# Modulation products in groups of four on TensorE, and other places in the order for three kinds of transfers

## The chip, the core and the metric

The kernel runs on one core of a Trainium2 chip. The core has a matrix engine (TensorE, PE in the profile, its weight loads as PEld), a vector engine (VectorE, DVE), an activation engine (ScalarE, ACT), a general engine (GpSimd, POOL) and a queue engine (SyncE, SP). Sixteen DMA engines move data between HBM and the on-chip memory SBUF; in this kernel transfers are issued from SP and from POOL. Products are accumulated in PSUM, from which DVE and ACT read. The metric is the device time of one execution in microseconds; lower is better.

## The reference

One inference step of a two-layer decoder trunk over a prompt of 1024 tokens and 8 single-token samples that share the weights (model width 1024). Cut to what matters here:

```python
for l in range(2):
    mod = silu(c) @ ada_w[l] + ada_b[l]              # c: 1 prompt row and 8 sample rows
    sh1, s1, g1, sh2, s2, g2 = split(mod, 6)         # each 1024 wide
    h = rmsnorm(x, norm_mix[l]) * (1 + s1) + sh1
    out, state = even_mixer(h) if l == 0 else mamba_mixer(h)
    x = x + g1 * out
    h = rmsnorm(x, norm_mlp[l]) * (1 + s2) + sh2
    x = x + g2 * (square(relu(h @ mlp_w1[l])) @ mlp_w2[l])      # hidden width 4096
y = rmsnorm(x, norm_final)
```

The even mixer has four HGRN2 heads of 128 channels, a gated linear recurrence. For the samples a head takes one recurrent step on a given state, once per sample:

```python
S = f[:, None] * S + (1 - f)[:, None] * v[None, :]   # S: 128 x 128 per head and sample
o = q @ S                                            # the new S is an output too
```

## The kernel before, in words

**Number format and large products.** Data is float32. A large product is made of three matmuls of rounded halves (lines 395 to 397, `mm3`): weight-high by data-high, weight-high by data-low, weight-low by data-high. `prep` loads a weight unit of 128x1024 on SP (`raw`, two buffers), ACT rounds it (`whi`) and DVE takes the rest (`wlo`); `need` hands out the next unit and keeps three more in preparation.

**Order.** The program is written as one sequence. The framework then places every instruction on its engine by a simulated schedule of its own, in which an instruction goes as soon as its inputs are there in the simulation; on the chip each engine then runs its list strictly in order. `tc.keep_in_program_order(i)` puts an instruction behind the one written just before it on the same engine. `dma` issues a transfer on SP; `dma_aux` (line 199) issues it on POOL and always pins it, so POOL's transfers keep the written order, and a transfer that has to wait holds all behind it. `Background` runs generators a step at a time between products, so that small work is written in between large work.

**Modulation** (`ada_gen`, line 251). Per layer three groups `g`, each of eight slices `k`. One slice is a group of four products, `j` = 0 to 3: the condition tile `ct` (128x32) is the weight, a tile of `ada_w` (128x512 float32, 256 KB) the data, and the result goes to 32 rows of one PSUM tile, so each `j` uses other 32 columns of the array. The float32 product shows as two MATMUL records on line 272. `load()` issues the four tiles of a slice on SP, one slice ahead; after eight slices ACT copies the sum (line 278), PE transposes it (line 281), DVE writes `mod`. `ada_steps(n)` advances the generator by n steps: 10 at the start, one with each weight unit that `need` hands out in the even mixer, 3 and then one with each of the first 16 products of the first half of an MLP, and one with each unit of its second half. Layer 1's modulation is made in layer 0's MLP; its last group (`g` = 2, `rest=1` holds back its first load) falls into the second half.

**MLP, first half** (from line 710). The hidden layer is computed with a seven-product scheme (Strassen's, Winograd's form) on 16 pairs `p` of weight tiles: `AOPS` lists 112 products `(p, q)`. Each is 24 matmuls into one of four PSUM tiles `pd`; DVE takes it out by lines 748 to 770, by `q`. Products 1 and 2 of the pairs in `SPLIT` (0 to 7, 14 and 15) run early, and product 1 of these is stored to HBM (`keep`, line 745) and loaded back (`kept`, line 704, into `saved`) for line 748, which is part of `q` = 6. `ff_out` (line 670) makes relu and square of a finished tile on ACT, splits it (lines 577 and 578), and stores it to `fd` in HBM on POOL. From pair 2 on the order within a pair is 6, 7, 5, 4, 3 (with 1 first and 2 after 5 where they did not run early). After products (14, 1) to (15, 2) come pairs 12 and 13 with all seven, then 14 and 15 with five each.

**MLP, second half** (line 783). Eight chunks of four `w2` units. A chunk reads eight tiles `ffc`, which `load_ff` loads from `fd` on POOL. Those of chunk 0 are loaded during the last 24 products of the first half, one with each product, into buffers (tag `hA`) that products 1 and 2 read until (13, 2).

**HGRN head** (`hgrn_gen`, line 825). For the first half of the tokens and the samples: `vd` (line 901) writes the samples' v to HBM in pieces of 4 bytes, `vb` (line 932) reads it back copied to all partitions; then for each half of the samples 256 KB of the old state `stt` is loaded (line 947), scaled by `f` on ACT (line 951), and added to on DVE (line 952); the result is stored (line 961). All this is issued on SP. Around it PE transposes (lines 898, 906), ACT copies (903, 908) and PE goes on with line 913.

Of the kernel before, what the change touches and what calls it, by code (L numbers as in the profile page):

```python
# [7 lines left out]
F32 = mybir.dt.float32  # L8
# [138 lines left out]
def kernel(ctx: ExitStack, tc: tile.TileContext, A: dict):  # L147
# [25 lines left out]
    def t2(w=W2, dt=F32):  # L173
        t = tp.tile([P, W2], dt, name="t2", tag="t2", bufs=N2)
        return t[:, :w]
# [20 lines left out]
    def dma(out, in_):  # L196
        nc.sync.dma_start(out=out, in_=in_)
# [53 lines left out]
    def ada_gen(l, alloc, rest=None):  # L251


        todo = [(12 * l + 4 * g, k) for g in range(3) for k in range(KT)]
        raws = []

        def load():
            if todo:
                i, k = todo.pop(0)
                rs = [alloc(512) for _ in range(4)]  # L260
                for j, raw in enumerate(rs):
                    dma(raw, A["ada"][i + j][:, k * 512:k * 512 + 512])
                raws.append(rs)
        load()
        yield
        for g in range(3):
            pt = psm()
            if not raws:
                load()
            for k in range(KT):  # L270
                for j, raw in enumerate(raws.pop(0)):
                    PE.matmul(pt[32 * j:32 * j + 32], ct[:, k], raw, start=k == 0, stop=k == KT - 1,
                              tile_position=(0, 32 * j))
                if (g, k) != (rest, KT - 1):
                    load()
                yield
            st = alloc(512)
            S.copy(st, pt)
            pm = psm()
            for q in range(4):  # L280
                PE.transpose(pm[:, q * P:q * P + P], st[:, q * P:q * P + P], ident)
            i0 = 48 * l + 16 * g
            V.tensor_add(mod[:, i0:i0 + 16, :].rearrange("p (j q) b -> p j q b", q=4),
                         pm.rearrange("p (q j b) -> p j q b", q=4, j=4)[:, :, :, 0:9],
                         vec("adab", i0, 16).rearrange("p (j q) -> p j q", q=4).unsqueeze(3)
                         .broadcast_to([P, 4, 4, 9]))
            yield
# [92 lines left out]
    def need(kind, idx):  # L380

        i = wpos[0]
        assert order[i] == (kind, idx), (i, order[i], kind, idx)
        wpos[0] += 1
        if kind[0] != "a":
            ada_steps(1)
        while len(units) <= min(i + AHEAD, max(i, limit[0] - 1)):
            units.append(prep(*order[len(units)]))
        u, units[i] = units[i], None
        return u  # L390
# [270 lines left out]
    def mlp(l, ctx_b, res, last, lorder=(3, 2)):  # L661
# [42 lines left out]
        def kept(p):  # L704

            if p in SPLIT and p not in saved:
                saved[p] = t3(HX)
                dma_aux(saved[p], keep[p])
# [5 lines left out]
        for i, (p, q) in enumerate(AOPS):  # L714
# [15 lines left out]
                stage[0] = None  # L730
            if q == 6:
                kept(p)
            elif q == 4 and p + 1 in keep:
                kept(p + 1)
            w = 512 * (n % 2), got[n // 2]
            m1, m2 = pair_tiles(p)
            pt = pd()
# [34 lines left out]
            if (p, q) == FRONT[1][-1]:  # L772
                ff0 = load_ff(0)
                ffs = next(ff0)
            elif ffs:
                next(ff0, None)
            bg.tick(2)
            if i < 2 * LEAD:
# [46 lines left out]
    def hgrn_gen(h, hf, st, carry, ff):  # L825

        n = HALF_N[hf]
        v4 = lambda a: a.rearrange("p (a t) -> p a t", t=P)
        v8 = lambda a: a.rearrange("p (a t) -> p a t", t=64)

        f = st.pop("f")
        V.tensor_scalar(f, f, lbo[:, h:h + 1], lbt[:, h:h + 1], op0=ALU.mult, op1=ALU.add)
# [65 lines left out]
            PE.transpose(pt[:, sb * P:sb * P + P], vt[:, sb * P:sb * P + P], ident)  # L898
        if hf == 0:
            vd = dr.tile([NS, P], F32, name="vd", tag="vd", bufs=2)  # L900
            dma(vd.rearrange("b p -> p b"), vt[:, 512:520])
        vn = vt[:, :512]
        S.copy(vn, pt)
        pt = psm()
# [20 lines left out]
                                       op0=ALU.mult, op1=ALU.add)  # L925
            carry["S"] = Sn
        if hf == 1:
            dma(A["o_hgp"][h], carry["S"])
        if hf == 0:
            vb = [t2(512), t2(512)]  # L930
            for qq in range(2):
                dma(vb[qq], vd[4 * qq:4 * qq + 4].rearrange("(o b) p -> o (b p)", o=1).broadcast_to([P, 512]))
        yield
        po = psm()
        for sb in range(4):
# [5 lines left out]
        yield  # L941
        if hf == 0:

            stts = []
            for qq in range(2):
                stt = t2(512)
                dma(stt, A["st_hg"][h][:, qq * 512:qq * 512 + 512])
                for bb in range(4):
                    b = 4 * qq + bb
                    c = slice(bb * P, bb * P + P)  # L950
                    S.mul(stt[:, c], stt[:, c], fs[:, b:b + 1])
                    V.scalar_tensor_tensor(stt[:, c], vb[qq][:, c], fs[:, 8 + b:9 + b], stt[:, c],
                                           op0=ALU.mult, op1=ALU.add)
                stts.append(stt)
                yield
            pq = psm()
            for b in range(NS):
                PE.matmul(pq[:, b:b + 1], stts[b // 4][:, (b % 4) * P:(b % 4) * P + P], qs[:, b:b + 1],
                          start=True, stop=True)
            for qq in range(2):  # L960
                dma(A["o_hgs"][h][:, qq * 512:qq * 512 + 512], stts[qq])
            S.copy(o[:, 512:520], pq[:, 0:8])

        while "g" not in st:
# [784 lines left out]
```

## Time and profile before

| | us |
|---|---|
| median of 3 runs | 2911.93 |
| lowest and highest | 2908.77 and 2917.14 |
| profiled execution | 2907.54 |
| its span, first to last instruction | 2905.8 |

In the profile's rows, "x" is a count, "<-" names what ended a wait or, between tile names, what was read for what was written. "busy" of PE counts a matmul until its modelled end, so matmuls overlap in it. A row of the view of waits gives the waiting engine, the line, what it waited for, the total in us, the times and the longest. A row of the timeline gives the start in us, the length, engine, line, operation, tiles, shapes and count, and in brackets the idle time before it and what ended it. A row of the view of stretches gives the stretch, its length, each engine's busy us with its count of instructions, PE's granted clock (1.00 is full), the DMA engines' busy share and GB/s.

The stages by the trace: the even mixer to about 570 us, layer 0's MLP to 1350 (first half to 961), the odd mixer to 2180, layer 1's MLP to the end (first half to 2527).

### The profile page before, as it was taken

To read this page: it belongs to the slowest core of one execution; us is meant where nothing else is said; L and a number is where in the kernel's file an instruction comes from. 1 tells how busy PE (TensorE), PEld (TensorE's weight loads), DVE (VectorE), ACT (ScalarE), POOL (GpSimd) and SP (SyncE) were. 2 spreads that over 40 slices of the span, in tenths; PEclk is the share of its full clock that TensorE was granted. 3 is DMA by queue.
4 is the path that set the end of the run, shared out by engine and by line. 5 is a ranking of instruction groups with operands and counts; after the bars stand their busy time and mean duration, and the time that the engine had idled before them with its cause. 6 is when DMAs were issued, how large, how long until landed. Compare 5 with 4: busy or idle time off the path is not lost. (4 is left out here: it accounts for less than half of the span.)

```text
span 2905.8 us, 47220 instructions
## 1 busy us (share of the span) xinstructions
PE 2771.9 (95%) x18636; PEld 2445.0 (84%) x18636; DVE 1854.9 (64%) x3712; ACT 1390.6 (48%) x2347; POOL 208.2 (7%) x356
## 2 busy tenths in 40 slices
PE   7999899999998899999889999999999999899998
PEld 3777788768998789999889897787779999899997
DVE  5646553666776334447689788998778766544446
ACT  4665522364555200015688776878756556301002
POOL 0000000011111200100000000000002111301100
PEclk9999999999999999999999999999999999999999
DMA  8642301296656943431656546443335655844431
GB/s 296 176 152 68 95 31 59 100 307 193 194 171 208 338 136 113 160 112 54 121 134 190 143 135 159 138 136 120 113 116 175 194 160 168 280 172 161 168 102 66
DMA packets 199933, 444.23 MB, mean 153 GB/s; under 512 B 35488, under 2 KB 53792, under 8 KB 199712
## 3 DMA queue, kind: packets, MB, share of 16 engines
q1 hardware_dynamic: 138144, 277.92, 32.2%
q0 software_dynamic: 61568, 163.29, 16.9%
q8 instruction: 147, 2.41, 0.3%
q14 instruction: 74, 0.61, 0.1%
HBM read 343.06 MB, written 98.08 MB: 152 GB/s over the span
## 5 line engine op out<-in xcount | busy, mean ns | idle before, releaser
L376 ACT CAST whi<-raw 128x1024 fp32r<-128x1024 f32 x228 | 238.1, 1046 | 826.3 <-PE pg L396 804.8
L505 DVE SCALAR_TENSOR_TENSOR x<-pg,mod,x 128x256 f32<-128x256 f32 (+1 forms) x576 | 326.3, 570 | 433.9 <-PE pg L397 428.5
L395 PE MATMUL pg<-hh,whi 128*128 128x264 f32 (+2 forms) x1656 | 546.5, 330 | 11.2 <-ACT xy L1203 5.4
L396 PE MATMUL pg<-hl,whi 128*128 128x264 f32 (+2 forms) x1656 | 533.2, 322 | 0.1
L397 PE MATMUL pg<-hh,wlo 128*128 128x264 f32 (+2 forms) x1656 | 532.8, 322 | 0.0
L395 PE MATMUL pg<-ffc,whi 128*128 128x256 f32 (+2 forms) x1488 | 476.9, 320 | 1.7 <-ACT t L577 1.7
L397 PE MATMUL pg<-ffc,wlo 128*128 128x256 f32 (+2 forms) x1488 | 477.6, 321 | 0.0
L396 PE MATMUL pg<-ffc,whi 128*128 128x256 f32 (+2 forms) x1488 | 476.6, 320 | 0.0
L377 DVE TENSOR_TENSOR wlo<-raw,whi 128x1024 fp32r<-128x1024 f32 x228 | 278.2, 1222 | 168.6 <-ACT whi L376 140.5
L395 PEld LDWEIGHTS pg<-hh,whi 128*128 128x128 f32 x1656 | 314.2, 190 | 53.7 <-issue 13.8
L396 PEld LDWEIGHTS pg<-hl,whi 128*128 128x128 f32 x1656 | 314.2, 190 | 31.5 <-issue 6.4
L397 PEld LDWEIGHTS pg<-hh,wlo 128*128 128x128 f32 x1656 | 313.5, 189 | 26.1 <-issue 2.1
L395 PE MATMUL pd<-hh,whi 128*128 128x258 f32 x1024 | 294.9, 288 | 26.2 <-DVE t L748 21.5
L395 PEld LDWEIGHTS pg<-ffc,whi 128*128 128x128 f32 x1488 | 280.5, 189 | 31.5 <-ACT whi L376 5.0
L397 PEld LDWEIGHTS pg<-ffc,wlo 128*128 128x128 f32 x1488 | 280.0, 188 | 25.3 <-issue 2.7
L396 PEld LDWEIGHTS pg<-ffc,whi 128*128 128x128 f32 x1488 | 279.8, 188 | 22.5 <-issue 0.2
L396 PE MATMUL pd<-hh,whi 128*128 128x258 f32 x1024 | 293.5, 287 | 0.0
L397 PE MATMUL pd<-hh,wlo 128*128 128x258 f32 x1024 | 291.6, 285 | 0.0
L395 PEld LDWEIGHTS pd<-hh,whi 128*128 128x128 f32 x1024 | 196.3, 192 | 42.3 <-issue 33.5
L396 PEld LDWEIGHTS pd<-hh,whi 128*128 128x128 f32 x1024 | 196.1, 191 | 12.0 <-issue 9.5
L397 PEld LDWEIGHTS pd<-hh,wlo 128*128 128x128 f32 x1024 | 196.4, 192 | 2.5 <-issue 2.5
L395 PE MATMUL pg<-ffh,whi 128*128 128x264 f32 (+2 forms) x544 | 176.4, 324 | 2.7 <-ACT bcz L1387 1.8
(291 smaller groups left out, 5299.8 us busy)
## 6 DMA issues: line engine op xcount, KB each, us to landing
raw<-W SPq DMA_DIRECT2D x314, 512.0 KB, 4.2
ffc<-fd POOLq DMA_DIRECT2D x128, 516.0 KB, 10.6
fd<-x POOLq DMA_DIRECT2D x106, 516.0 KB, 4.1
t<-ada SPq DMA_DIRECT2D x192, 256.0 KB, 5.2
t<-csd SPq DMA_DIRECT2D x64, 256.0 KB, 4.8
fd<-t POOLq DMA_DIRECT2D x44, 258.0 KB, 4.9
x<-xd POOLq DMA_DIRECT2D x16, 516.0 KB, 9.9
t<-st_ss SPq DMA_DIRECT2D x32, 256.0 KB, 4.5
```

The source lines that it names most:

```text
L376: S.copy(hi, raw)
L377: V.tensor_sub(lo, raw, hi.bitcast(F32))
L395: PE.matmul(pt, wh, xh, start=first and i == 0, stop=False)
L396: PE.matmul(pt, wh, xl, start=False, stop=False)
L397: PE.matmul(pt, wl, xh, start=False, stop=last and i == n - 1)
L505: V.scalar_tensor_tensor(x[:, m, s:s + npr], pt[:, :npr], mod[:, self.gi + m, 0:1], x[:, m, s:s + npr], op0=ALU.mult, op1=ALU.add)
```

## The change

It has five parts.

1. The four products of a slice are written in the order `j` = 3, 0, 1, 2, and the last three are pinned behind the one written before.
2. `ada_steps` is not called with the first eight units of an MLP's second half, so that layer 1's last modulation group begins with chunk 2 in place of chunk 0.
3. `kept`: the load for pair p+1 is written at product (p, 6) and no longer at (p, 4), and only for p above 1. For p = 2 the load stands at (2, 6) itself, together with that for pair 3; before, it stood at (1, 4). A load at (0, 4) whose result was read by nothing is gone.
4. The eight `ffc` tiles of chunk 0 are loaded with every second product and no longer with each.
5. In a HGRN head the old state is one tile of 512 KB (`hst`, one buffer), loaded at the head's beginning; it, `vd`, `vb`, the new state (now one store) and the prompt's end state are issued on POOL. ACT's and DVE's work on the state is the same, written to the one tile.

```diff
@@ -268,9 +268,12 @@
             for k in range(KT):
-                for j, raw in enumerate(raws.pop(0)):
-                    PE.matmul(pt[32 * j:32 * j + 32], ct[:, k], raw, start=k == 0, stop=k == KT - 1,
-                              tile_position=(0, 32 * j))
+                rs = raws.pop(0)
+                for j in (3, 0, 1, 2):
+                    mm = PE.matmul(pt[32 * j:32 * j + 32], ct[:, k], rs[j], start=k == 0, stop=k == KT - 1,
+                                   tile_position=(0, 32 * j))
+                    if j < 3:
+                        tc.keep_in_program_order(mm)
@@ -382,7 +385,7 @@
-        if kind[0] != "a":
+        if kind[0] != "a" and (kind[:2] != "w2" or idx >= 8):
             ada_steps(1)
@@ -730,8 +733,8 @@
             if q == 6:
                 kept(p)
-            elif q == 4 and p + 1 in keep:
-                kept(p + 1)
+                if p > 1 and p + 1 in keep:
+                    kept(p + 1)
@@ -772,7 +775,7 @@
-            elif ffs:
+            elif ffs and i % 2:
                 next(ff0, None)
@@ -827,6 +830,9 @@
+        if hf == 0:
+            stt = ph.pool.tile([P, NS * P], F32, name="hst", tag="hst", bufs=1)
+            dma_aux(stt, A["st_hg"][h])
@@ -898,7 +904,7 @@
-            dma(vd.rearrange("b p -> p b"), vt[:, 512:520])
+            dma_aux(vd.rearrange("b p -> p b"), vt[:, 512:520])
@@ -925,11 +931,11 @@
         if hf == 1:
-            dma(A["o_hgp"][h], carry["S"])
+            dma_aux(A["o_hgp"][h], carry["S"])
         if hf == 0:
             vb = [t2(512), t2(512)]
             for qq in range(2):
-                dma(vb[qq], vd[4 * qq:4 * qq + 4].rearrange("(o b) p -> o (b p)", o=1).broadcast_to([P, 512]))
+                dma_aux(vb[qq], vd[4 * qq:4 * qq + 4].rearrange("(o b) p -> o (b p)", o=1).broadcast_to([P, 512]))
@@ -941,24 +947,18 @@
-            stts = []
             for qq in range(2):
-                stt = t2(512)
-                dma(stt, A["st_hg"][h][:, qq * 512:qq * 512 + 512])
                 for bb in range(4):
                     b = 4 * qq + bb
-                    c = slice(bb * P, bb * P + P)
+                    c = slice(b * P, b * P + P)
                     S.mul(stt[:, c], stt[:, c], fs[:, b:b + 1])
-                    V.scalar_tensor_tensor(stt[:, c], vb[qq][:, c], fs[:, 8 + b:9 + b], stt[:, c],
+                    V.scalar_tensor_tensor(stt[:, c], vb[qq][:, bb * P:bb * P + P], fs[:, 8 + b:9 + b], stt[:, c],
                                            op0=ALU.mult, op1=ALU.add)
...
-            for qq in range(2):
-                dma(A["o_hgs"][h][:, qq * 512:qq * 512 + 512], stts[qq])
+                PE.matmul(pq[:, b:b + 1], stt[:, b * P:b * P + P], qs[:, b:b + 1], start=True, stop=True)
+            dma_aux(A["o_hgs"][h], stt)
```

More of the change, by code (lines that the diff above doesn't have):

```diff
@@ L942, in hgrn_gen @@
         if hf == 0:
-            stts = []
             for qq in range(2):
-                stt = t2(512)
-                dma(stt, A["st_hg"][h][:, qq * 512:qq * 512 + 512])
                 for bb in range(4):
                     b = 4 * qq + bb
-                    c = slice(bb * P, bb * P + P)
+                    c = slice(b * P, b * P + P)
                     S.mul(stt[:, c], stt[:, c], fs[:, b:b + 1])
-                    V.scalar_tensor_tensor(stt[:, c], vb[qq][:, c], fs[:, 8 + b:9 + b], stt[:, c],
+                    V.scalar_tensor_tensor(stt[:, c], vb[qq][:, bb * P:bb * P + P], fs[:, 8 + b:9 + b], stt[:, c],
                                            op0=ALU.mult, op1=ALU.add)
-                stts.append(stt)
                 yield
@@ L957, in hgrn_gen @@
             for b in range(NS):
-                PE.matmul(pq[:, b:b + 1], stts[b // 4][:, (b % 4) * P:(b % 4) * P + P], qs[:, b:b + 1],
-                          start=True, stop=True)
-            for qq in range(2):
-                dma(A["o_hgs"][h][:, qq * 512:qq * 512 + 512], stts[qq])
+                PE.matmul(pq[:, b:b + 1], stt[:, b * P:b * P + P], qs[:, b:b + 1], start=True, stop=True)
+            dma_aux(A["o_hgs"][h], stt)
             S.copy(o[:, 512:520], pq[:, 0:8])
```

## The prediction, made before the changed kernel was run

> **What bounds the kernel now.** I read the page first: the sum per engine, then the view of PE's waits.
>
> ```profile
> span 2905.8 us, 47220 instructions
> PE 2771.9 (95%) x18636; PEld 2445.0 (84%) x18636; DVE 1854.9 (64%) x3712; ACT 1390.6 (48%) x2347; POOL 208.2 (7%) x356
> ```
> ```profile
> PE pd L395 <- DVE t L748: 23.0, 4, 9.6
> PE psm L913 <- ACT t L908: 15.0, 2, 9.0
> PE psm L272 <- DMA t<-ada: 12.6, 7, 4.8
> ```
>
> PE is the bound, 95% busy, with every other engine far below. What can go is PE's idle time, 2905.8 - 2771.9 = 134 us, and PE work that is arranged badly. Three of the largest waits are at places that the change touches: line 748 (kept products), line 913 (a HGRN head, behind ACT) and line 272 (modulation tiles not landed). PE's own price per product is read from its timeline, a lone modulation product first, then a whole group of four (two records each), and from a stretch without any:
>
> ```profile
> 577.48 0.39 PE L395 MATMUL pd<-hh,whi 128*128 128x258 f32 x1
> 577.79 1.04 PE L272 MATMUL pm<-t,ct 128*32 128x512 f32 x2
> 578.77 0.39 PE L396 MATMUL pd<-hh,whi 128*128 128x258 f32 x1
> ```
> ```profile
> 625.26 0.28 PE L397 MATMUL pd<-hh,wlo 128*128 128x258 f32 x1
> 625.48 1.06 PE L272 MATMUL pm<-t,ct 128*32 128x512 f32 x8
> 626.48 0.39 PE L395 MATMUL pd<-hh,whi 128*128 128x258 f32 x1
> ```
> ```profile
> 574.00:668.00 94.00, 93.28 (x523) 54.98 (x524) 60.75 (x81) 54.73 (x87) 16.13 (x29) 0.98 0.94 312
> 14.00:40.00 26.00, 24.07 (x87) 6.12 (x88) 6.56 (x19) 5.69 (x12) 0.00 (x0) 1.00 0.98 360
> 970.00:990.00 20.00, 15.98 (x58) 7.16 (x59) 3.01 (x5) 1.05 (x1) 6.36 (x12) 0.84 1.10 403
> 790.00:840.00 50.00, 49.79 (x416) 49.61 (x415) 31.22 (x50) 28.32 (x50) 6.86 (x10) 1.00 0.56 163
> ```
>
> Without modulation a matmul takes 49.79/416 = 0.12 us, a seven-product step of 24 takes 2.87. With the lone product the next start comes 578.77 - 577.48 = 1.29 after the one before, with the group of four 626.48 - 625.26 = 1.22; less 0.12 they cost 1.17 and 1.10. Four products beside each other cost what one costs: **1.15 us a piece, however many of a group stand in it**.
>
> **Part 1, groups of four.** The pieces are counted in PE's timeline; the first and the last of two stretches:
>
> ```profile
> 45.30 2.38 PE L272 MATMUL psm<-t,ct 128*32 128x512 f32 x6
> ...
> 201.58 1.04 PE L272 MATMUL psm<-t,ct 128*32 128x512 f32 x2
> ...
> 574.04 3.51 PE L272 MATMUL pm<-t,ct 128*32 128x512 f32 x6 [2.91 <-DVE x L604]
> ...
> 662.65 4.11 PE L272 MATMUL pm<-t,ct 128*32 128x512 f32 x10
> ```
>
> From 45 to 203 there are 21 pieces for 14 groups, from 574 to 668 34 for 16. The pins make 0, 1 and 2 follow 3, whose tile is issued last, so each group becomes one piece. Even mixer: seven pieces fewer; that at 45 lies beside PE's start, where it waits for its data anyway, so 6 x 1.15 = **6.9 us**. First half of the MLP: 18 x 1.15 = 20.7 us of PE work goes. But there the cover is thin: the DMA engines are at share 0.94. The stretch moves 94 x 312 = 29.3 MB. At the 403 GB/s of the row from 970 this takes 72.7 us, at the 360 of the row from 14 81.4, at its own 312 per 0.94, so 332, 88.3. The gain lies between 94 - 88.3 = 5.7 and the whole 20.7; I take the row from 14, which carries the same tiles: **12.6 us**. What is late next there is a tile of `ada`.
>
> **Part 2, the last group of layer 1.** In chunk 0 PE meets tiles just issued, while the DMA engines are at share 1.10:
>
> ```profile
> 972.35 3.81 PE L272 MATMUL psm<-t,ct 128*32 128x512 f32 x4 [4.79 <-DMA t<-ada]
> 976.10 0.58 PE L397 MATMUL pg<-ffc,wlo 128*128 128x256 f32 x1
> ...
> 984.30 1.05 PE L272 MATMUL psm<-t,ct 128*32 128x512 f32 x4
> ...
> 989.05 0.39 PE L395 MATMUL pg<-ffc,whi 128*128 128x256 f32 x1
> ```
>
> The wait of 4.79, then 976.10 - 972.35 - 0.98 = 2.8 within the first piece (0.98 is a piece's own length, 577.79 to 578.77), then 989.05 - 984.30 - 0.98 = 3.8 in the second group: 11.4 us. The first slice is in three pieces, so 2 x 1.15 more goes. In chunk 2 the first slice is again loaded in the same step as its products, but the burst of loads that opens the second half is over (the calm stretch from 790 has share 0.56); a wait there is between 0 and 4.8, I take half: 11.4 + 2.3 - 2.4 = **11.3 us**.
>
> **Parts 3 and 4, kept products and `ffc`.** Layer 0 on POOL, DVE and PE:
>
> ```profile
> 914.31 1.63 POOL L201 DMA_DIRECT2D ffc<-fd  x3 [30.08 <-PE pd L397]
> ```
> ```profile
> 932.23 0.70 DVE L578 TENSOR_TENSOR x<-t,x 128x516 fp32r<-128x516 f32 x1 [2.59 <-ACT x L577]
> 934.94 0.70 DVE L578 TENSOR_TENSOR x<-t,x 128x516 fp32r<-128x516 f32 x1 [2.01 <-ACT x L577]
> ...
> 936.92 1.90 DVE L373 TENSOR_TENSOR wlo<-t,whi 128x512 fp32r<-128x512 f32 x3
> 940.13 0.69 DVE L748 TENSOR_TENSOR t<-t,pd 128x516 f32<-128x516 f32 x1 [1.32 <-DMA t<-kept]
> ```
> ```profile
> 940.97 0.55 PE L395 MATMUL pd<-hh,whi 128*128 128x258 f32 x1 [9.59 <-DVE t L748]
> 941.32 0.42 PE L396 MATMUL pd<-hh,whi 128*128 128x258 f32 x1
> 941.53 0.42 PE L397 MATMUL pd<-hh,wlo 128*128 128x258 f32 x1
> ```
>
> POOL stands 30 us with the first `ffc` load at its head, which needs the buffer of (13, 2); all behind it goes out in a burst, and pair 14's kept load is the fifteenth in it, behind eight `ffc` and six `fd`. It lands at 940.13: (940.13 - 914.31)/15 = 1.72 us a place. By the new written order (`ffc` with odd products, the kept load at (13, 6), not (13, 4)) it is the ninth, at about 930. The wait of POOL stays. DVE is late itself, though: the two `L578` wait for stores that free their slots, in the eighth and tenth place before, the fifth and seventh after, some 5 us earlier. Without the kept load DVE is free at 936.92 + 1.90 = 938.8; 5 us earlier it starts line 748 near 934.6 instead of 940.13. I take **5.5 us** per layer (the view of waits has the same row in layer 1: 23.0 in 4, two of them near 9.6), between 1.3 (DVE no earlier) and the whole 9.6. After the wait PE runs slower: 0.21 us a matmul, not 0.12, for one product of 24, 2.2 us. By the Trainium skill, "TensorE: Matmul & The Clock Gate", Part 1 (What's actually happening), an idle window of about 3.4 us drops PE to half its clock; the trace agrees (0.21 to 0.12). By this rule the 4 us of wait that I leave would still cost these 2.2, and only a wait cut below 3.4 would add 2 x 2.2 to the gain; the sum takes nothing.
>
> Against this stands the load for pair 2, now at its own product. Layer 1:
>
> ```profile
> 2271.80 1.38 POOL L201 DMA_DIRECT2D fd<-x  x2 [5.04 <-DVE x L578]
> ```
> ```profile
> 2276.72 0.28 PE L395 MATMUL pd<-hh,whi 128*128 128x258 f32 x1
> ```
> ```profile
> DMA to landing us min/median/max: 2.8/4.7/10.0
> ```
>
> It comes behind these two stores, at about 2272.9, and lands by the kept loads' median at 2277.6. DVE waits at line 748 with all its queue; PE needs that tile of four at its 31st product, 2276.72, and gets it at 2277.6 + 0.7 + 0.1. 1.7 us, and I take 1.8 per layer, between 0 and 7 (the longest landing). Pairs 3 to 7 get their loads earlier and had no wait. Together 2 x (5.5 - 1.8) = **7.4 us**.
>
> **Part 5, HGRN heads.**
>
> ```profile
> ACT t L951 <- DMA t<-st_hg: 16.0, 2, 9.0
> ```
> ```profile
> 144.05 0.38 SPq L197 DMA_DIRECT2D vd<-t  x1
> 144.53 2.58 SPq L197 DMA_DIRECT2D t<-ada  x4
> ```
> ```profile
> 155.99 5.36 PE L272 MATMUL psm<-t,ct 128*32 128x512 f32 x8 [4.67 <-DMA t<-ada]
> ```
>
> In heads 2 and 3 ACT waits 16.0 us in all for the state, which SP issues only after `vd` has landed; the copies of lines 903 and 908 stand behind it, and PE at line 913 behind these, 15.0 us. Loaded at the head's start, the state is there, and what is left is a copy of 0.6 each: **13.8 us** (lower bound 7, if DVE, which still waits for `vb` at line 952, delays ACT; upper 18 with the slow clock after). Six issues per head come to POOL, idle in this stage; new waits there (`vb` for `vd`, a state for the store before it) hold only each other.
>
> In head 1 four `ada` loads are issued right behind `vd` and PE waits 4.67 and then within the piece 5.36 - 1.06 = 4.3. Moved to another queue, `vd` may leave these loads free or not; no POOL transfer stands beside a `vd` in this trace. Between 0 and 9.0 I take half, **4.5 us**.
>
> **Sum**: 6.9 + 12.6 + 11.3 + 7.4 + 13.8 + 4.5 = 56.5 us off the profiled execution's 2907.5. It lies 4.4 us under the median of 2911.9, from which I take the sum: **2855 us**, 2.0%.
>
> **The rivals.** *`vd` clogs all engines wherever it is issued*: its 4-byte pieces hold the 16 engines, the 4.5 stays, and `vb` comes no earlier, so DVE in heads 2 and 3 gives half of 13.8 back: 2911.9 - (56.5 - 4.5 - 6.9) = 2867. For it: one set of 16 engines is all there is to share. The Trainium skill says so, "DMA: Bandwidth & Descriptors", Issuing engines are not separate DMA queues: issuing elsewhere saves only issue time. No run here shows it yet.
>
> *Transfers set the pace from 574 to 668*: 5.7 in place of 12.6 there, only 8.9 in chunk 2 (a wait of 4.8), 1.3 per layer in place of 5.5, no 4.5: 2911.9 - (6.9 + 5.7 + 8.9 - 1.0 + 13.8) = 2878. For it speaks the share of 0.94, against it the whole group at 625, beside which PE had no wait.
>
> *The change doesn't do what it says*: a pin gives an order, not a neighbour, and other matmuls slip in between. Then 6.9, 12.6 and 2.3 go: 2877. The chain 3, 0, 1, 2 leaves little room for it: once 3 is placed, the other three are ready.
>
> *Slower: PE waits for the last of four tiles.* Before, each product went when its own tile was there; now PE stands until the fourth of a group has landed, and all four buffers come free at once, so the next loads start late. Place: the 38 groups behind PE's start. It decides from 56.5/38 = 1.5 us a group; at 2.0 the time is 2911.9 - 56.5 + 76 = 2931. For it speaks that PE waited 12.6 us for such tiles already; against it that groups of eight records, as at 625, stand in the trace without a wait.
>
> **How the numbers follow.** Forecast 0.52, clogging 0.13, transfers 0.12, not together 0.05, gains mostly given back by new waits (within 0.3%, about what a measurement of this kernel can tell from no change, 8.7 us) 0.09, slower 0.09. Faster 0.82, same 0.09, slower 0.09. With every term at its upper bound (6.9 + 20.7 + 13.7 + 19.2 + 18 + 9.0) the time is 2824, with every one at its lower (6.9 + 5.7 + 8.9 - 11.4 + 7 + 0) 2895; this is the range, and it leaves out the last two cases.
>
> **What would show it.** Right: modulation pieces of eight records throughout, fewer than 50 of them; no `DMA t<-st_hg` among ACT's waits, line 913 under 2 us; line 272 not at 972; PE's wait for line 748 near 4 us instead of 9.6 in both layers, and a new one of 1 to 3 us about four products after (2, 6). Wrong: waits of PE for `ada` that grow past 20 us, DVE waiting at line 952 so that weights come late, or a stretch from the even mixer's end to i = 16 that is as long as before with PE idle in it.

## The result and the profile after

| | before | after |
|---|---|---|
| median, us | 2913.69 | 2897.45 |
| lowest and highest of 4 runs | 2908.77 and 2917.14 | 2892.55 and 2900.79 |
| profiled execution, us | 2907.54 | 2900.04 |

The ratio is 0.9944, 95% interval 0.9921 to 0.9967: faster, by 16 us where 56.5 were forecast; the time lies 2 us above the upper end of the range. One execution of `rows_no_1_5`, 8994 us, and one of the kernel before in the runs further down, 5405 us, were in a slow state and are left out of the ratios. The first lines of the profile's page after the change, then rows of its view of PE's waits (engine, line, what ended the wait, us in total, times, longest; lines 273, 398 and 751 are 272, 395 and 748 of before):

```profile
span 2898.2 us, 47219 instructions
PE 2743.0 (95%) x18636; PEld 2448.9 (84%) x18636; DVE 1855.8 (64%) x3712; ACT 1390.0 (48%) x2346; POOL 221.0 (8%) x378
```
```profile
PE psm L273 <- DMA t<-ada: 20.8, 8, 9.6
PE pm L273 <- DMA t<-ada: 15.5, 8, 3.7
PE pd L398 <- DVE t L751: 12.0, 7, 3.1
PE pg L398 <- issue: 9.6, 2, 5.3
PE pd L398 <- ACT whi L375: 7.0, 4, 3.3
PE psm L919 <- ACT t L914: 2.5, 2, 2.0
```

PE is busy 28.9 us less (2771.9 before), yet the span shrinks by only 7.6: saved work became waiting. The wait at line 748 fell from 23.0 to 12.0 and that behind the HGRN copies from 15.0 to 2.5; the one for tiles of `ada` rose from 12.6 to 20.8 + 15.5 = 36.3. By stages, each from the first matmul of one to that of the next, read from both timelines (the two profiled executions are 7.5 us apart where the medians are 16, so the stages explain half of what was measured):

| stage, us | before | after | gain | forecast |
|---|---|---|---|---|
| start to layer 0's first product (even mixer) | 577.5 | 575.5 | 2.0 | 6.9 + 13.8 + 4.5 |
| products 0 to 16, layer 0 | 90.4 | 89.2 | 1.2 | 12.6 |
| product 16 to second half, both layers | 293.6 + 297.9 | 297.9 + 300.9 | -7.3 | 7.4 |
| second half, layer 0 | 389.4 | 377.1 | 12.3 | 11.3 |

The rest (odd mixer, layer 1's first products and second half) differs by 0.7 us. One stage came as forecast, three did not: the even mixer lacks 23.2 us of its forecast, the products from 16 on 14.7, and products 0 to 16 11.4.

**Products 0 to 16.** The view of stretches (us, PE, PEld, DVE, ACT, POOL busy with counts, granted clock, DMA share, GB/s), and one of the new waits in PE's timeline:

```profile
574.00:665.00 91.00, 74.69 (x523) 54.68 (x516) 60.06 (x78) 52.63 (x83) 16.36 (x29) 0.88 0.92 313
580.00:660.00 80.00, 65.64 (x473) 50.03 (x472) 51.66 (x66) 45.93 (x70) 15.81 (x28) 0.91 0.97 330
```
```profile
647.39 1.06 PE L273 MATMUL pm<-t,ct 128*32 128x512 f32 x8 [2.29 <-DMA t<-ada]
648.38 0.52 PE L398 MATMUL pd<-hh,whi 128*128 128x258 f32 x1
648.70 0.42 PE L399 MATMUL pd<-hh,whi 128*128 128x258 f32 x1
648.91 0.42 PE L400 MATMUL pd<-hh,wlo 128*128 128x258 f32 x1
...
655.55 1.93 PE L273 MATMUL pm<-t,ct 128*32 128x512 f32 x8 [3.23 <-DMA t<-ada]
```

The 16 groups stand in 15 pieces, where 34 were. In the starts of successive matmuls, modulation takes 17.8 us of PE in place of 35.5, and idle time 16.3 in place of 0.7. Between 580 and 660 the DMA engines are at 0.97, and the tiles come no faster. They are also asked for late. SP's issues of the tiles that PE waits for at 647.39 and 655.55, and a row of SP's waits from 575 to 665:

```profile
642.27 2.88 SPq L197 DMA_DIRECT2D t<-ada  x4
648.46 9.36 SPq L197 DMA_DIRECT2D t<-ada  x6
```
```profile
SPq L197 <- PE pm L273: 24.0, 14, 3.5
```

The first load of each row goes out as soon as a group of PE (those that start at 641.19 and 647.39 and last 1 us) has freed its buffer. The tiles waited for at 647.39, 655.55 and 661.17, 9.2 of the 15.5 us, were issued within 0.5 us of the end of the group before, and landed 3.6 to 6.6 us later.

**Even mixer.** SP's and POOL's issues, and the DMA view's lines of the two kinds of small stores (tile, queue, count, KB each, median us from issue to landing):

```profile
155.84 0.90 POOL L201 DMA_DIRECT2D vd<-t  x1 [13.24 <-ACT sm L245]
166.55 1.09 POOL L201 DMA_DIRECT2D t<-vd  x2 [9.81 <-DMA vd<-t]
```
```profile
156.60 0.33 SPq L197 DMA_DIRECT2D raw<-W  x1
157.03 8.57 SPq L197 DMA_DIRECT2D t<-ada  x6
```
```profile
bcd<-bcz SPq DMA_DIRECT2D x8, 4.0 KB, 14.3
vd<-t POOLq DMA_DIRECT2D x4, 4.0 KB, 10.1
```

4 KB take 10 us, and the `ada` tiles that SP issues in that time land only at 171.7 to 173.5; PE waits 9.59 us for them at 173.57. The queue was changed, the sixteen engines are the same. The DVE view holds what became of ACT's wait for the state:

```profile
DVE hst L955 <- DMA t<-vd: 16.9, 3, 8.7
```

**End of the first half.** POOL's timeline in layer 0:

```profile
916.46 0.55 POOL L201 DMA_DIRECT2D ffc<-fd  x1 [30.07 <-PE pd L400]
...
921.23 0.85 POOL L201 DMA_DIRECT2D t<-kept  x1
```
```profile
935.03 0.36 PE L398 MATMUL pd<-hh,whi 128*128 128x258 f32 x1 [1.50 <-DVE t L751]
...
941.40 0.39 PE L398 MATMUL pd<-hr,whi 128*128 128x258 f32 x1 [3.26 <-ACT whi L375]
...
942.56 0.58 PE L400 MATMUL pd<-hr,wlo 128*128 128x258 f32 x1 [0.65 <-DVE wlo L376]
```
```profile
938.70 0.69 DVE L340 TENSOR_TENSOR t<-raw 128x512 f32<-128x512 f32 x1 [3.01 <-DMA raw<-W]
```

Pair 14's kept load goes out in the ninth place, as forecast, and the wait of 9.59 is now 1.50. But a weight unit's load lands late (DVE's row), so PE waits for that unit (3.26 + 0.65), and the second half starts 4.28 late: 9.7 us in all.

### The profile page after: what moved, and what is told of

It is laid out like the page before. It is cut to its first block, busy times and chain, and to the rows that moved or that the text cites. A ratio compares the mean times of both kernels' runs of the same rounds, so it can differ in the third digit from the quotient of the medians.

```text
span 2898.2 us, 47219 instructions
## 1 busy us (share of the span) xinstructions
PE 2743.0 (95%) x18636; PEld 2448.9 (84%) x18636; DVE 1855.8 (64%) x3712; ACT 1390.0 (48%) x2346; POOL 221.0 (8%) x378
## 3 DMA queue, kind: packets, MB, share of 16 engines
q0 software_dynamic: 63456, 169.34, 17.7%
## 5 line engine op out<-in xcount | busy, mean ns | idle before, releaser
L398 PE MATMUL pg<-hh,whi 128*128 128x264 f32 (+2 forms) x1656 | 545.9, 330 | 11.5 <-ACT whi L379 4.4
```

The lines of the kernel that those rows point to most:

```text
L398: PE.matmul(pt, wh, xh, start=first and i == 0, stop=False)
```

## Experiments

Two theories ran through them. **A**: PE's gains were turned into waits for transfers, those behind the 4-byte stores and those of the stretch from 574 us. **B**: the parts are worth what was forecast and the loss lies in how they meet. Each ratio is against the kernel before on the same chip (medians 2906.4 to 2909.0). The result's own kernel before has 2913.69, so a run is set beside the changed kernel by its ratio (0.9944) rather than by its median.

### Each part alone

The edits are parts 1, 2, 3 with 4, and 5 of the diff above, each alone.

> The kernel before with part 1 alone: the four products of a slice in the order 3, 0, 1, 2, pinned. Theory A (a group waits for all four tiles, and from 574 to 668 us the transfers set the pace): the even mixer gains a few us of pieces and gives some back at its start, layer 0's first 16 products stay near 90 us (90.4 before), so 3 to 9 us faster in all. Theory B (each part is worth what was forecast, and the parts disturb each other): 6.9 in the even mixer, 12.6 in the 94 us, 2.3 in the second half, so 20 to 24 us faster, with the 16 products in 74 to 84 us.

> The kernel before with part 2 alone: no step of the modulation with the first eight units of an MLP's second half. Theory A and the prediction agree on its place: the two waits in chunk 0 of layer 0 go. Without the groups the 2.3 us of pieces stay: 8 to 10 us faster, all of it between the start of layer 0's second half and the odd mixer. If the waits come again with chunk 2: within 3 us of the kernel before.

> The kernel before with parts 3 and 4 alone: kept loads at (p, 6) for p+1, the loads for pairs 2 and 3 at (2, 6), ffc loads with every second product. Theory A (the 30 us for which POOL stands with an ffc load at its head, and the burst after it, stay; the late load for pair 2 costs on its own): 3 to 10 us slower, products 16 to 35 longer by 4 to 7 us in layer 0 and 2 to 3 in layer 1, line 748 at 935 us short, but about 8 us of waits after it per layer. Theory B (the forecast): 7.4 us faster.

> The kernel before with part 5 alone: a head's state in one tile loaded at its beginning, and all of the head's transfers on POOL. Both theories: ACT's wait for st_hg goes and line 913 waits under 4 us in place of 15.0, so 11 to 14 us. Theory A (vd holds the DMA engines from POOL as it did from SP): the waits for modulation tiles behind it stay at 8 us or more, 7 to 13 us faster in all. Theory B (the other queue leaves these loads free): waits for modulation tiles under 6 us, 15 to 20 us faster.

| | median, us | ratio, 95% interval |
|---|---|---|
| p1_groups | 2920.24 | 1.0047 (1.0031 to 1.0064) |
| p2_rest | 2895.24 | 0.9957 (0.9944 to 0.9970) |
| p34_kept_ffc | 2910.45 | 1.0010 (0.9997 to 1.0024) |
| p5_hgrn | 2907.99 | 1.0001 (0.9991 to 1.0011) |

**Part 1** is a loss of 11.5 us, which neither theory expected. By stages, from the first large product to the MLP takes 540.5 us in place of 532.8 and the second half 395.2 in place of 389.4, while products 0 to 16 take 4.1 less. Rows of its view of waits, and the stretches at PE's start and around 574 us, first of part 1 alone, then of before:

```profile
PE psm L273 <- DMA t<-ada: 33.6, 10, 8.6
PE pm L273 <- DMA t<-ada: 14.7, 8, 3.5
```
```profile
20.00:50.00 30.00, 17.62 (x82) 3.01 (x74) 13.40 (x29) 8.17 (x13) 0.00 (x0) 0.66 1.00 365
565.00:690.00 125.00, 103.06 (x712) 80.69 (x712) 87.53 (x136) 68.51 (x110) 18.78 (x33) 0.90 0.74 262
```
```profile
20.00:50.00 30.00, 24.59 (x87) 5.86 (x80) 14.97 (x33) 9.20 (x15) 0.00 (x0) 0.94 1.00 367
565.00:690.00 125.00, 118.92 (x711) 78.99 (x710) 85.00 (x122) 66.59 (x107) 16.95 (x30) 0.99 0.78 257
```

48.3 us of waits for `ada` stand where 12.6 were, and the clock falls in both stretches (0.94 to 0.66, 0.99 to 0.90). Lone products had gone one by one as their tiles landed, and the clock stayed up. From 20 to 50 us it is 0.89 to 0.95 in all eight kernels of this document with lone products, and 0.59 to 0.72 in all twelve with groups. **Part 2** brings 13.5, more than the 8 to 10 expected and all at its place (389.4 to 375.5 us); it also takes away the chunk in which part 1 alone waits 8.6 and 7.2 us. **Parts 3 and 4** bring nothing: products 16 to 35 grow by 5.2 and 3.4 us. In layer 0 that is theirs (57.3 to 60.7 us in the six kernels without them, 62.7 with them); in layer 1 it is not shown to be (61.2 to 64.6 without, 64.7 with). **Part 5** alone makes the even mixer 10.2 us shorter from its first large product on (532.8 to 522.7), and line 913's successor waits 2.0, as both theories had it. The waits for modulation tiles did not fall, as theory A had it: 7.4 us at 165.71, in place of 5.7. But the time is unchanged, which neither expected. The first large product came 2.5 us later, and about 8.5 us came back at places it does not touch (line 748 27.8 us in 7 waits, not 23.0 in 4; line 372 5.6 in 6, not 1.9 in 2), with PE's instructions from product 35 to 87 in the same order. Why those loads land later stays open.

The four sum to about -1 us, the change to -16. In the second half part 1 costs 5.8 alone and part 2 brings 13.9, together 12.3 are kept; the rest of the difference is not settled.

### Mechanisms, on the changed kernel

```diff
-            dma_aux(vd.rearrange("b p -> p b"), vt[:, 512:520])
+            pv = psm()
+            PE.transpose(pv[0:NS, 0:P], vt[:, 512:520], ident)
+            vs = ph.pool.tile([NS, P], F32, name="vs", tag="vs", bufs=1)
+            S.copy(vs, pv[0:NS, 0:P])
+            dma_aux(vd, vs)
```

> The changed kernel, but PE transposes the samples' v of a head (128x8) before it is stored, so that vd goes out in 8 rows of 512 bytes in place of 1024 pieces of 4 bytes, still on POOL. Theory A (the 4-byte pieces hold all 16 engines for some 10 us whichever queue issues them, and the modulation tiles behind them land late): PE's waits of 3.9 and 9.6 us at 92 and 174 us go, DVE gets vb some 8 us sooner, 10 to 15 us faster than the changed kernel. Theory B (a group waits because its four tiles and their buffers come late, whatever vd does): these waits stay within 3 us, and so does the time.

```diff
-                rs = [alloc(512) for _ in range(4)]
-                for j, raw in enumerate(rs):
+                rs = [alloc(512)] * 4 if l else [alloc(512) for _ in range(4)]
+                for j, raw in enumerate(rs[:1] if l else rs):
```

> The changed kernel, but in layer 1's modulation (made in layer 0's MLP) one tile of ada_w serves all four products of a slice, so that a slice loads 256 KB in place of 1 MB; the modulation values of layer 1 are other ones, and the work of PE is the same. Theory A (from 574 to 668 us the transfers set the pace): products 0 to 16 of layer 0 take 70 to 76 us in place of 89.2, 14 to 20 us faster in all. Theory B (PE waits because all four buffers come free at once and the next loads start late, or because of DVE and ACT): 84 us or more, under 6 us faster.

```diff
-            if (p, q) == FRONT[1][-1]:
+            if i == 103:
...
-            elif ffs and i % 2:
+            elif ffs:
```

This starts the eight loads with product 104, so they stand with 104 to 111, four products later than its expectation says.

> The changed kernel, but the eight ffc loads of chunk 0 are written with products 100 to 107, one each, after (13, 2), the last reader of their buffers. Theory A (POOL's stand of 30 us and the burst behind it are the cause of the waits near the end of the first half): POOL stands no longer, the waits after 935 us in layer 0 (1.5, 3.3, 0.7, 4.3) and their like in layer 1 go but for 1 to 2 us, 7 to 9 us per layer, 14 to 18 us faster than the changed kernel. Theory B (the stores of fd and the raw loads alone fill the engines there, or the ffc tiles now land too late): PE waits for ffc or raw at the start of the second half, and the time is within 5 us.

```diff
-            if i < 2 * LEAD:
-                ada_steps(1)
...
-        ada_steps(3)
...
-        if kind[0] != "a" and (kind[:2] != "w2" or idx >= 8):
-            ada_steps(1)
+        if kind[:2] == "w2":
+            ada_steps(int(idx >= 4))
+        elif kind[0] != "a":
+            ada_steps(1)
```

> The changed kernel, but layer 1's modulation is made wholly in the second half of layer 0's MLP, a slice with each unit from the fifth on, in groups as before. Theory A (the first half cannot take these transfers, share 0.92 and more, the second half at share 0.4 can): products 0 to 16 of layer 0 fall from 89 to about 51 us, the second half grows by 16 pieces of 1.15 us and gets no wait for ada, 17 to 22 us faster than the changed kernel. Theory B (the modulation costs the same wherever it stands, since it takes transfers from the raw loads there): the second half grows by 30 us or more, within 6 us of the changed kernel.

| | median, us | ratio, 95% interval | the stage in question, us (changed kernel) |
|---|---|---|---|
| vd_rows | 2884.25 | 0.9911 (0.9894 to 0.9928) | first large product to MLP 514.9 (528.2) |
| one_tile | 2871.38 | 0.9867 (0.9849 to 0.9886) | products 0 to 16: 65.5 (89.2) |
| ffc_late | 2918.82 | 1.0035 (1.0024 to 1.0046) | 102 to second half 29.7 and 29.7 (40.6 and 42.6) |
| mod_second_half | 2892.04 | 0.9940 (0.9923 to 0.9957) | 0 to 16: 59.3 (89.2); second half 399.2 (377.1) |

`vd_rows` went to theory A: by the ratios it is 0.33% faster than the changed kernel, 9.6 us. The DMA view's line of the store:

```profile
vd<-vs POOLq DMA_DIRECT2D x4, 4.0 KB, 1.6
```

The same 4 KB from the same queue land in 1.6 us, and the 9.59 us wait is 0.4. `one_tile`, with a quarter of layer 1's modulation bytes and the same PE work, went further than theory A asked: the stretch falls by 23.7 us, and no wait for a modulation tile is left in it. So the loads of these tiles set the pace there. The run does not say whether by their bytes or by the buffers they wait for, since it needs a quarter of both. `ffc_late` shows both sides: the end of the first half is 11 and 13 us shorter, and PE stands 2.1 us (layer 0) and 9.8 us (layer 1) for `ffc` tiles that now come late. Besides, the framework placed layer 1's last modulation group into chunk 0, with waits of 6.0, 12.2 and 7.7 us for its tiles. `mod_second_half` lies between the theories: 29.9 us gained, 22.2 given back in the second half, and a ratio that its interval does not part from the changed kernel's.

### Around the store in rows

All four are `vd_rows` with one more edit. The first takes part 1 out. The second writes the kept load for pair 2 where the kernel before has it. The third begins the `ffc` loads of chunk 0 behind (13, 2):

```diff
-            if (p, q) == FRONT[1][-1]:
+            if (p, q) == (13, 2):
...
-            elif ffs and i % 2:
-                next(ff0, None)
+            elif ffs:
+                for _ in range(2):
+                    next(ff0, None)
```

The fourth advances the modulation with every second of the first 16 products, and starts the second group in the second half.

> The kernel of vd_rows without part 1: lone modulation products in the order 0 to 3, nothing pinned, each when its own tile is there. Theory A (grouping saves pieces of 1.15 us only where the tiles are there early, and behind PE's start and from 574 to 668 us it turns the time saved into waits): first product of a large unit 2 to 3 us sooner than with groups (47.1), even mixer some 7 us longer after that, products 0 to 16 of layer 0 near 90 us (87.1 with groups), second half of layer 0 2 to 6 us longer: 5 to 12 us slower than vd_rows (2884). Theory B (the groups are a loss as in the run of part 1 alone): faster than vd_rows by 3 us or more.

> The kernel of vd_rows, but the kept load for pair 2 is written at (1, 4) again, where the kernel before has it. Theory A (at (2, 6) it lands after DVE asks for it, and DVE's queue and PE wait): products 16 to 35 fall from 62.1 to 57 to 59 us in layer 0 and from 61.8 to about 61 in layer 1, 3 to 6 us faster than vd_rows. Theory B (those products wait for the stores and raw loads beside it whatever its place): within 2 us of vd_rows.

> The kernel of vd_rows, but the eight ffc loads of chunk 0 are written with the four products right after (13, 2), two with each, so that POOL never stands with one at its head. Theory A (the stand of 30 us and its backlog make the waits near the end of the first half): products 102 to the second half's start take 29 to 32 us in place of 40.1 (layer 0) and 42.4 (layer 1), ffc tiles are there in time, 12 to 20 us faster than vd_rows. Theory B (the same bytes in fewer us starve the raw loads, or the tiles land late as in ffc_late): PE waits for whi or ffc instead, and the time is within 5 us of vd_rows or above it.

> The kernel of vd_rows, but only the first group of layer 1's modulation (8 of 24 slices) is made in the first half, a slice with every second of the first 16 products; the other two groups stand in the second half from chunk 2 on. Theory A (from 574 to 668 us the transfers set the pace, and a third of these tiles fits beside the rest): products 0 to 16 of layer 0 fall from 87.1 to 56 to 64 us, the second half grows by 8 pieces, 9 to 12 us, 12 to 20 us faster than vd_rows. Theory B (transfers cost the same in either half): the sum of both stages stays within 5 us.

| | median, us | ratio, 95% interval |
|---|---|---|
| vd_rows_lone | 2886.88 | 0.9915 (0.9898 to 0.9932) |
| vd_rows_kept2 | 2879.65 | 0.9899 (0.9882 to 0.9916) |
| vd_rows_ffc_burst | 2854.28 | 0.9807 (0.9791 to 0.9823) |
| vd_rows_one_group | 2877.44 | 0.9887 (0.9870 to 0.9903) |

Without part 1 the time is the same within its interval: neither theory's number came, the groups are worth nothing measurable here. The kept load for pair 2 is 4.6 us by the medians, which the intervals do not part from none; products 16 to 35 of layer 0 fall from 62.0 to 59.5, near theory A's 57 to 59, and in layer 1 nothing was gained (62.9 after 61.8). The `ffc` loads were the find: 30 us, 23.2 of them between product 102 and the second half by the profiles. POOL's timeline in the same place:

```profile
906.36 0.67 POOL L201 DMA_DIRECT2D fd<-x  x1 [1.15 <-DVE x L581]
906.92 1.25 POOL L201 DMA_DIRECT2D ffc<-fd  x2
910.89 0.68 POOL L201 DMA_DIRECT2D fd<-x  x1 [2.73 <-DVE x L581]
911.46 1.20 POOL L201 DMA_DIRECT2D ffc<-fd  x2
912.52 0.69 POOL L201 DMA_DIRECT2D t<-kept  x1
913.05 2.27 POOL L201 DMA_DIRECT2D ffc<-fd  x4
```

No `ffc` load waits for PE, stores and kept loads go out between, and from product 102 on 29.7 us pass in both layers (40.2 and 42.4 in `vd_rows`), with no wait of PE over 0.9 us. One group in the first half is worth 6.8 us by the medians, not 12 to 20: 15.5 gained in products 0 to 16, 9.6 given back in the second half.

### What was left open, and the best kernel

`before_rows` is the kernel before with `vd` in rows on SP, `before_ffc_burst` the kernel before with the `ffc` edit. `together` joins the four edits above to the changed kernel. `together_bc_rows` also treats the odd mixer's stores (`bcd`) as `vd`:

```diff
-            dma(d.rearrange("b p -> p b"), o.bcz[:, par + i, 512:520])
+            pv = psm()
+            PE.transpose(pv[0:NS, 0:P], o.bcz[:, par + i, 512:520], ident)
+            vs = ph.pool.tile([NS, P], F32, name="bcs", tag="bcs", bufs=1)
+            S.copy(vs, pv[0:NS, 0:P])
+            dma(d, vs)
```

> The kernel before, with nothing of the change, but vd stored in 8 rows of 512 bytes after a transpose on PE, on SP as before. Theory A (the 4-byte pieces are what held the transfers behind vd): ACT's wait for st_hg falls from 16.0 us to under 6, the waits for modulation tiles in the even mixer go, and the even mixer falls from 532.8 to 515 to 524 us, 8 to 16 us faster than before. Theory B (the place of the state's load on SP, behind vd and vb, made the wait): ACT still waits 10 us or more for st_hg, under 5 us faster.

> The kernel before with one edit: the eight ffc loads of chunk 0 are written with the four products after (13, 2), two with each. Theory A (POOL's stand of 30 us is the cause by itself): the wait of 9.6 us at line 748 goes in both layers, products 102 to the second half's start fall from 41.8 and 42.0 us to 29 to 32, and the time by 18 to 25 us. Theory B (it needs the kept loads of part 3 or the free POOL of part 5): 34 us or more there, under 10 us faster.

> The changed kernel with vd in rows, the kept load for pair 2 at (1, 4), the ffc loads right behind (13, 2) and one group of layer 1's modulation in the first half. If the gains of the single runs (13.2, 4.6, 30.0 and 6.8 us) add up: 2843 us, between 2837 and 2850. If the ffc burst or the modulation in the second half take transfers from each other: 2852 or more.

> The kernel of together, but the odd mixer's eight stores of the samples' B and C, also 1024 pieces of 4 bytes each, go out in rows of 512 bytes after a transpose on PE. Theory A (pieces of 4 bytes hold the engines there as well, and PE waits behind DVE and ACT for csd and state loads): the odd mixer, 829 us, falls by 4 to 15 us. Theory B (there PE's waits come from DVE's own work, with the transfers hidden): within 3 us of together.

> The kernel before with part 2, the kept loads of part 3 (that for pair 2 at (1, 4)), the ffc loads right behind (13, 2), and both kinds of 4-byte stores in rows of 512 bytes; without parts 1 and 5. Theory A (parts 1 and 5 only shifted the price of the 4-byte stores, and part 5 now costs): even mixer 505 to 510 us in place of 516.9, products 0 to 16 of layer 0 near 90, 2812 to 2822 us, faster than together_bc_rows (2826). Theory B (both parts have their worth once the stores are out of the way): 2832 us or more.

> The kernel of rows_no_1_5 with part 1 added. Theory A (a group saves pieces and waits for its last tile as long): within 4 us of rows_no_1_5, products 0 to 16 of layer 0 still over 84 us. Theory B (with transfers free the forecast's 6.9 and 12.6 us come): 10 us or more faster than rows_no_1_5.

| | median, us | ratio, 95% interval |
|---|---|---|
| before_rows | 2884.52 | 0.9913 (0.9897 to 0.9929) |
| before_ffc_burst | 2901.32 | 0.9970 (0.9954 to 0.9985) |
| together | 2852.20 | 0.9806 (0.9791 to 0.9822) |
| together_bc_rows | 2826.15 | 0.9714 (0.9698 to 0.9730) |
| rows_no_1_5 | 2816.03 | 0.9682 (0.9666 to 0.9699) |
| rows_no_5 | 2813.16 | 0.9675 (0.9657 to 0.9693) |

`before_rows` decides the first open point for the pieces. One store in rows, nothing else, gives 23.7 us, more than theory A expected and more than the whole change; the even mixer falls from 532.8 to 507.5. Its waits of ACT for the state and of PE for modulation tiles (none of these in the even mixer behind its first large product, 5.7 us there before):

```profile
ACT t L955 <- DMA t<-st_hg: 2.8, 2, 2.6
```
```profile
PE psm L272 <- DMA t<-ada: 6.9, 4, 4.7
PE pm L272 <- DMA t<-ada: 0.6, 1, 0.6
```

The state still stands behind `vd` and `vb` on SP, and ACT waits 2.8 us where it waited 16.0. With the rows, part 5 costs: `vd_rows_lone` has the same even mixer with part 5 and takes 517.5. There DVE waits 21.4 us for `vb` (16.9 in the changed kernel), and `before_rows` has no such wait; PE waits behind DVE for 5.1 us at line 946 of that kernel, 0.2 at the same line of `before_rows`. That covers half of the 10 us; the rest is not shown.

`before_ffc_burst` lies between the theories: from product 102 to the second half 36.9 and 36.2 us, not 29.7, because line 748 still waits 4.6 and 3.9 us for kept loads. Parts 3 and 4 alone left 40.5 and 40.4 there. Of the edits tried, only the kept loads at (p, 6) together with `ffc` loads behind (13, 2) take the wait away.

`together` does not add up: 2852 where 2843 was expected. Beside the `ffc` edit, one group and the early kept load give 2 us, not 11. In `together_bc_rows` the odd mixer falls by 28.2 us (828.9 to 800.7). ACT's waits there for the transfers behind those stores, first in `together`, then in `together_bc_rows`:

```profile
ACT t L1378 <- DMA t<-st_ss: 24.7, 12, 7.7
ACT t L1296 <- DMA t<-csd: 24.3, 7, 7.0
```
```profile
ACT t L1382 <- DMA t<-st_ss: 15.0, 11, 2.6
ACT t L1296 <- DMA t<-csd: 11.3, 7, 3.5
```

`rows_no_1_5` and `rows_no_5` went to theory A: without part 5 the even mixer is 506.9 and 505.9, and part 1 makes a difference of 3 us, which the intervals do not part from none. `rows_no_5` is the fastest here, 0.9675 of the kernel before.

## Why the prediction was wrong

The largest miss is in the even mixer, 25.2 us forecast and 2.0 measured, where the sum had no term for the price of the store ahead of the loads. After it come the kept and `ffc` loads, and products 0 to 16.

- **A piece costs 1.15 us, however many products** held nearly: 15 pieces in place of 34 took 17.7 us off PE from 574 to 668, 0.93 a piece. In the even mixer the groups came to 18 pieces, not 14, because matmuls slip between two products of one group (a pin orders, it does not join, as the third rival said; eight of the 18 hold four records): 3 pieces fewer after 45 us, 3 x 1.15 = 3.5, not 6.9.
- **12.6 from 574 to 668** failed: 1.2. The bounds were right in kind, from transfers, but the value was taken from the row at 14 us (360 GB/s), and the stretch had its own, 312 at share 0.94; the lower bound of 5.7 set the engines busy throughout, and in the run the share stayed at 0.92. The rival "transfers set the pace" names one cause; the slower rival's mechanism, four buffers freed at once and the next loads issued late, stands beside it in the trace, and no run parts the two.
- **11.3 for part 2** held (12.3 in the change; 13.9 alone).
- **7.4 for parts 3 and 4** failed: -7.3. The price at (2, 6) was forecast at 1.8 a layer; products 16 to 35 cost 7.1 and 2.7. Moving that one load back gave 2.6 in layer 0 and nothing in layer 1, so the rest stays open. At the end the wait at line 748 fell as forecast (1.50 and 2.31, even below the 4 forecast). But the sentence "the wait of POOL stays" was passed over: its backlog made the next weight unit and the second half's start late, and took 8.2 us back in layer 0. The step did not ask what is late next.
- **6.9, 13.8 and 4.5 in the even mixer**: 25.2 forecast, 2.0 measured. The 13.8 held within its bounds of 7 and 18: part 5 alone gives 10.2 us from the first large product on. The 4.5 did not come, since PE waits 7.4 us for the tiles behind `vd` where it waited 4.7. The 6.9 turned into a loss of 7.6 with part 1 alone, whose groups wait 2.1, 0.4 and 8.4 us for their tiles. Together 4.6 are left, and 2.6 of these go because the first large product starts at 47.3 in place of 44.6; kernels without groups start it anywhere from 44.3 to 47.2, so this is not shown to be the change's. What the sum had at nothing was the store ahead of the loads, 1024 pieces of 4 bytes: ACT's wait was read as the place of a load in a queue, the load was moved, the store was not mended, and the wait went to DVE (16.9) and to PE's tiles (9.59). The rival "`vd` clogs all engines wherever it is issued" had it. The rule of the Trainium skill beside it ("DMA: Bandwidth & Descriptors", Issuing engines are not separate DMA queues) agrees with this trace: 10.1 us from POOL, and 9.59 of waiting for tiles issued on SP.
- **The slower rival** (PE waits for the last of four tiles) got 9 in 100. Part 1 alone shows it at work, 11.5 us slower; part 2 takes away 15.8 us of these waits (8.6 and 7.2 in chunk 0), which hid the loss in the change.
- **The rivals were priced as alternatives.** Nothing kept clogging and pacing from holding at once. Rival one takes 11.4 from the sum, rival two 22.2 (56.5 - 34.3), 4.5 of them the same: with both, 2911.9 - (56.5 - 29.1) = 2884.5. By stages the two still leave 13.8 for the even mixer, 5.7 for products 0 to 16 and -1.0 for parts 3 and 4. Measured were 2.0, 1.2 and -7.3, so the loss by the groups in the even mixer and the waits of parts 3 and 4 lie outside both.
- **The clock.** The prediction let a wait cost 2.2 us of half clock only from about 3.4 us on, by the Trainium skill's "TensorE: Matmul & The Clock Gate", Part 1 (What's actually happening). Here a wait of 2.29 (at 647.39) is followed by matmuls of 0.21 us for some 3 us, and so is one of 2.31 in layer 1 (at 2490.70); one of 1.50 (at 935.03) is not, nor one of 2.28 in the odd mixer (at 1523.69), so the length of the wait alone does not decide. The Trainium skill's 3.4 us is not a lower limit here, and the measurement decides. Of PE's waits for modulation tiles in the changed kernel behind its start, all six from 2.29 us up (2.29 to 9.59) stand in or next to a stretch at half clock, so they cost more than their length.

Its own list of signs was good: waits for `ada` past 20 us, DVE waiting at line 952, and a stretch to i = 16 as long as before with PE idle in it, were named as what would show it wrong, and all three came (36.3, 16.9 and 16.3 us).

## What to carry to other kernels

Before saving an engine's work, ask of that very stretch whether transfers leave it room, and when the buffers of the next ones come free: here, at a DMA share of 0.94, 17.7 us of work saved came back as 16.3 us of waiting. Ask also what the small work did for the clock while it filled a wait. When a transfer is late, look at what was issued just before it on any queue, and at its piece size, before moving it to another queue. A queue that stands had to be freed at its head here; respacing what is behind it moved the wait.

## What the runs showed that was not expected

- A store of 4 KB in pieces of 4 bytes lands 10.1 us (`vd`) or 14.3 us (`bcd`) after its issue, in rows of 512 bytes after 1.6 (`vd`). Twelve of them stood in the program; the four `vd` were worth 23.7 us in the kernel before, the eight `bcd` 26 in `together`.
- Matmuls slow to 0.21 us, from 0.12, after some waits as short as 2.29 us.
